# Gate products, single-token expert lists and input squares moved between stages and engines of a hybrid decoder block

## Chip, cores and metric

One core of one Trainium2 chip runs the whole block. The metric is device microseconds from start to end; lower is better. The time before is 1631.74 us, the median of 3 runs (1631.34 to 1634.24).

## What is computed

One layer for 256 tokens of width 2048, all in float32 at the interface:

```python
xn = rms_norm(x)
q, k, v, z, xbc, dt = split(xn @ w_in)
attn = rms_norm(stick_breaking_attention(rms_norm(q), rms_norm(k), v))
y = group_rms_norm(ssd_scan(silu(conv(xbc)), dt, ...) * silu(z))
h = x + concat(attn, y) @ w_out
hn = rms_norm(h)
q = (hn @ w_query).reshape(t, 8, 2, 128)
top_s, top_i = top_k(q . sub_keys, 16)          # per head and half
gate, expert = softmax(top16(top_s0 + top_s1)), key pair of 16384
out = h + sum_e gate_e * gelu(hn . expert_down[e]) * expert_up[e]
```

The last line is what the change touches most: each of the 256 tokens picks 16 of 16384 experts for each of 8 heads, and every expert has one row of 2048 numbers in `expert_down` and one in `expert_up`.

## The kernel before

Nothing is gathered per token. After the query the kernel sorts the used experts into **lists** of 128 experts each; one indirect DMA (L1355) brings a list's 128 rows of 2048 numbers, 1.05 MB, into SBUF. There are kinds of lists by how many tokens use an expert. A list of many-token experts is multiplied against tokens on TensorE (PE) after its rows have been transposed there. An expert that one token alone uses needs just one dot product; 30 lists hold such experts, and they are called **D lists** here.

The program is one long list `items`. `stream` walks over it: for each item it first issues the front part of the items a few places ahead (loads, transposes), then the item's matmuls, then a tick that advances every background generator in `bg` by one step and counts down the callbacks in `due`. The order of each engine's instructions follows from this walk and from the tile scheduler, which may still move them. The stages are:

1. Input projections: x arrives in 8 loads, ACT (L343) and VectorE (DVE, L344) split it with its gain into a rounded part and a rest, ACT and DVE (L222, L227) do the same with weights, and PE multiplies (L312, L313, L318). The mean square of x comes from four `Square`s of a quarter each (L2034, L2036), three sums (L2039) and a matmul. `squares` does two squares and two sums on GpSimd (POOL), two squares on ACT and one sum on DVE. Of the constant tables, two are loaded by POOL's own DMA queue (L422 and L428, together 0.66 MB).
2. Attention and scan, output projection, query, top-16 selection, listing.
3. **C units**, 20 lists of 4 items each, PE only on long matmuls (L1540 to L1542). Beside them runs `gates`: it turns the chosen experts and weights into a dense table of gates, 4 tokens at a time: one-hot tiles on DVE and POOL (L1246 to L1249), a product on PE (L1256), a copy on ACT (L1259), and at each half eight stores to a DRAM table `g_dram` (L1264). `GR` is how many such groups start per item. The expert rows go into a ring of five slots.
4. **T units**, 22 of them (numbered from 0 here), each a pair of lists in 8 items: transposes (L1465), ACT and DVE splits (L1442, L1443), matmuls (L1482 to L1484). Beside them run three things. `turn_hn` transposes the normalised hidden state (64 transposes, L1641) from unit `HU`; `form` fetches a list's gates from `g_dram` (L1420) and multiplies them in, from unit `GU`; and from unit `DU` on, `DN` D lists are zipped into T units. For a D list, `d_prep` fetches the gates, `find` (L1563 to L1565, 5 items later) finds on DVE which token each expert belongs to, `turn_` makes a one-hot matrix of it, 8 matmuls (L1609) pick the right token's hidden state for each row, and 4 DVE operations (L1615) form the dot products with the gathered rows.
5. The **D/up stage** (1182 to 1340 us): four more ring slots open (`begin`), and the D lists that are left are mixed with the first 29 lists of `expert_up` rows, whose halves ACT and DVE split (L1828, L1829) and PE multiplies into the output (L1895).
6. The late up lists, the same without D lists, to the end.

Row gathers, gate fetches and POOL's other work share POOL's one instruction stream. A row gather waits for a ring slot, and everything behind it on POOL waits with it. The gathers come in the order of the list `gathers`: the pair of a T unit, then a D list's rows, then the next pair. The few lines that set the order:

```python
HU, GU, DU, DN = 5, 9, 11, 11       # T unit of turn_hn, of form, first unit with a D list; D lists in T units
        n = i - DU
        if 0 <= n < DN:
            u = [x for p in zip(u[:4], dus[n]) for x in p] + u[4:]
    for n in range(DLOOK):
        after(1 + 3 * n, lambda n=n: d_prep(n))
```

Of the kernel before, what the change touches and what calls it, by code (L numbers as in the profile page):

```python
# [13 lines left out]
AF = mybir.ActivationFunctionType  # L14
OP = mybir.AluOpType
# [54 lines left out]
BASE = [sum(CAPS[:k]) for k in range(LC + 1)]  # L70
# [20 lines left out]
YR = 2  # L91
YC = 2
YT = 2
GR = 0.8
KP = 0
GW = 3
GLAG = 1
# [1 line left out]
OLAG = 7  # L99
TF = 10  # L100
XZ = 16
HU = 5
GU = 9
DU = 11
DN = 11
NPG = 4
YF = 3
HNP = 16
# [35 lines left out]
def tile_block(ctx: ExitStack, tc: tile.TileContext, xT, w_f, w_v, w_dt, w_o, w_q, sk, dnt, down, up,  # L144
               cols, hcols, cst, sel, sel2_, out):
    nc = tc.nc
# [63 lines left out]
    bg = []  # L210
# [46 lines left out]
    def after(n, fn):  # L257
        due.append([n, fn])
# [981 lines left out]
    def gates():  # L1240
# [32 lines left out]
        while t0 < T or q:  # L1273
            if gens.get("put"):
                gens["put"].pop(0)()
                yield from rest(GW if t0 < T else GX)
                continue
            credit += GR
            while q and (len(q) > GLAG or t0 == T):
# [39 lines left out]
    ts_ = plain[:TF] + buffered + plain[TF:]  # L1319
# [19 lines left out]
    gathers = []  # L1339
# [209 lines left out]
    d_list = sorted(d_of, key=d_of.get)  # L1549
# [157 lines left out]
    t_mark = len(items)  # L1707
    u_mark = []
    dus = [unit_d(k, r) for _, k, r in ds_]
    for i, (_, k, r) in enumerate(ts_):  # L1710
        u_mark.append(len(items))
        u = unit_t(k, r)
        n = i - DU
        if 0 <= n < DN:
            u = [x for p in zip(u[:4], dus[n]) for x in p] + u[4:]
        items.extend(u)
        if 0 <= n - 1 < DN:
            gathers.append(("down", d_list[n - 1]))
        gathers += [("down", BASE[k] + r + x) for x in range(2)]
    if len(ts_) - DU <= DN:  # L1720
        gathers.append(("down", d_list[len(ts_) - DU - 1]))
    d_mark = len(items)


# [281 lines left out]
    sqw = [slot(1, 1024 * q, 1024) for q in range(4)]  # L2006
# [23 lines left out]
    def squares():  # L2030
        for q in range(4):
            xq = xt_t[:, 1024 * q:1024 * (q + 1)]
            if q < 2:
                nc.gpsimd.tensor_tensor(sqw[q], xq, xq, op=OP.mult)  # L2034
            else:
                nc.scalar.activation(sqw[q], xq, AF.Square)  # L2036
                yield
            if q:
                (nc.gpsimd if q < 3 else nc.vector).tensor_tensor(sqw[0], sqw[0], sqw[q], op=OP.add)  # L2039

    sq_ = squares()
    next(sq_)
    bg.append(sq_)
    for k, n in enumerate(CL):
        after(n, lambda k=k: load_consts(k))
    stream(items, wo_mark)
# [14 lines left out]
    bg.append(gens["hnt"])  # L2061
    stream(items, u_mark[GU])
    while gens["hnt"] in bg:
# [2 lines left out]
    gens["form"] = form()  # L2066
    bg.append(gens["form"])
    for n in range(DLOOK):
        after(1 + 3 * n, lambda n=n: d_prep(n))
    stream(items, d_mark, d_mark)  # L2070
    pgs.extend(pg_all[NPG:])
    begin()
# [90 lines left out]
```

## Time and profile before

| | |
|---|---|
| median of 3 runs | 1631.74 us |
| profiled execution, its time | 1630.61 us |
| its span in the profile | 1628.7 us |
| TensorE busy | 1580.7 us, 97% |
| VectorE busy | 1156.0 us, 71% |
| ScalarE busy | 779.5 us, 48% |
| GpSimd busy | 531.1 us, 33% |
| mean granted clock | 0.997 |
| moved by DMA | 366.70 MB, mean 225 GB/s |

The profiled execution is the one from which all durations come. Its time is 1.9 us longer than the span that the profile covers, and 1.1 us below the median of the runs. An engine's share is an average over stages with different limits, so the views by stage and the waits say more than the table.

### The profile page before, as it was taken

What the parts mean: (1) busy time and instruction counts of PE and PEld (TensorE: products, weight loads), DVE (VectorE), ACT (ScalarE), POOL (GpSimd) and SP (SyncE); (2) the same over time, 40 slices, a digit from 0 to 9 for tenths busy, and PEclk for the clock granted to TensorE, in tenths of its full rate; (3) what the DMA queues carried; (4) which work ended last, traced back from release to release, by engine and by line L of the source; (5) the groups of instructions that cost most, each with busy time, mean ns of one, the idle gap of its engine ahead of it and who ended that gap; (6) DMA issues with size and microseconds to landing.
All of it is one profiled execution on the core that took longest, in us unless ns stands there. A gap on an engine that the chain in (4) does not pass through costs nothing. (4 is left out here: it accounts for less than half of the span.)

```text
span 1628.7 us, 27340 instructions
## 1 busy us (share of the span) xinstructions
PE 1580.7 (97%) x10330; PEld 1402.2 (86%) x10331; DVE 1156.0 (71%) x2556; ACT 779.5 (48%) x1375; POOL 531.1 (33%) x499
## 2 busy tenths in 40 slices
PE   6999999999999999999999999999998999999997
PEld 6999978999888888889999999999975468887776
DVE  7776665864487988736645774677797457888896
ACT  6554457754111200415545566655552036667664
POOL 3001100211000000034423431455576555786851
PEclk9999999999999999999999999999999999999999
DMA  6654544667745534253294269678799998898893
GB/s 207 188 163 151 156 155 141 183 201 225 244 143 149 164 90 119 66 198 120 96 292 171 79 229 340 227 288 307 284 398 413 356 383 332 322 347 304 327 334 115
DMA packets 108808, 366.70 MB, mean 225 GB/s; under 512 B 12704, under 2 KB 48800, under 8 KB 82304
## 3 DMA queue, kind: packets, MB, share of 16 engines
q0 software_dynamic: 35504, 229.43, 37.7%
q1 hardware_dynamic: 70304, 134.23, 27.0%
q8 instruction: 83, 1.36, 0.3%
q10 hardware_dynamic: 2864, 1.24, 0.3%
q14 instruction: 53, 0.43, 0.1%
HBM read 337.24 MB, written 27.92 MB: 224 GB/s over the span
## 5 line engine op out<-in xcount | busy, mean ns | idle before, releaser
L1895 PE MATMUL out<-hi_up,p 128*128 128x512 f32 x716 | 194.0, 392 | 0.7 <-DVE p L1797 0.6
L1355 POOL DMA_INDIRECT raws<-in_down,idx x71 | 72.3, 1018 | 303.8 <-DVE colt L1196 161.9
L1895 PEld LDWEIGHTS out<-hi_up,p 128*128 128x128 f32 x716 | 133.8, 188 | 30.7 <-ACT hi_up L1828 1.5
L253 PE MATMUL dn<-xt_t,raw_dn 128*128 128x256 f32 x640 | 158.3, 383 | 0.1
L1443 DVE TENSOR_TENSOR t<-tp,t 128x512 fp32r<-128x512 f32 x176 | 120.0, 688 | 48.3 <-ACT t L1442 47.6
L1420 POOL DMA_INDIRECT raw_small<-g_dram,idx x111 | 123.5, 1113 | 43.5 <-issue 28.7
L1442 ACT ACTIVATE t<-tp 128x512 fp32r<-128x512 f32 x176 | 103.8, 602 | 59.7 <-PE tp L1465 57.0
L253 PEld LDWEIGHTS dn<-xt_t,raw_dn 128*128 128x128 f32 x640 | 115.2, 193 | 11.7 <-issue 0.5
L253 PE MATMUL pq<-hg,raw_pq 128*128 128x256 f32 x512 | 112.9, 379 | 0.0
L253 PEld LDWEIGHTS pq<-hg,raw_pq 128*128 128x128 f32 x512 | 96.3, 190 | 12.5
L1259 ACT ACTIVATE big<-g 128x128 f32<-128x128 f32 x256 | 70.8, 438 | 75.8 <-PE g L1256 75.8
L1248 POOL TENSOR_TENSOR B<-B,gi 128x512 bf16<-128x512 bf16 x64 | 69.7, 1091 | 91.1 <-DVE B L1246 89.9
L1465 PE MATMUL tp<-ident,raws 128*128 128x128 f32 x544 | 95.5, 273 | 2.2 <-DVE t L1443 2.2
L1540 PE MATMUL zc<-hnl,c 128*128 128x256 f32 x320 | 95.9, 300 | 0.0
L1828 ACT ACTIVATE hi_up<-raws 128x1024 fp32r<-128x1024 f32 x74 | 77.1, 1056 | 32.7 <-PE out L1895 29.3
L1542 PE MATMUL zc<-hnl,c 128*128 128x256 f32 x320 | 89.1, 278 | 0.0
L1541 PE MATMUL zc<-hnl,c 128*128 128x256 f32 x320 | 89.0, 278 | 0.0
L1828 ACT ACTIVATE hi_up<-rows_hn 128x1024 fp32r<-128x1024 f32 x68 | 71.1, 1059 | 34.7 <-PE out L1895 29.4
L1443 DVE TENSOR_TENSOR c<-tc,c 128x512 fp32r<-128x512 f32 x80 | 55.2, 691 | 43.3 <-ACT c L1442 43.3
L1249 DVE TENSOR_TENSOR A<-O,gi 128x1024 f16<-128x1024 bf16 x64 | 47.4, 741 | 52.0 <-PE g L1256 51.8
L1829 DVE TENSOR_TENSOR lo_up<-rows_hn,hi_up 128x1024 fp32r<-128x1024 f32 x58 | 71.2, 1234 | 13.3 <-ACT hi_up L1828 10.5
L1355 POOL DMA_INDIRECT rows_hn<-in_up,idx x48 | 63.0, 1312 | 46.7 <-DVE lo_up L1829 12.9
(540 smaller groups left out, 4628.4 us busy)
## 6 DMA issues: line engine op xcount, KB each, us to landing
raw_dn<-in_dnt SPq DMA_DIRECT2D x40, 512.0 KB, 3.9
raw_kq<-in_w_f SPq DMA_DIRECT2D x32, 512.0 KB, 3.8
raw_wo<-in_w_o SPq DMA_DIRECT2D x32, 512.0 KB, 4.5
raw_pq<-in_w_q SPq DMA_DIRECT2D x32, 512.0 KB, 3.8
g_dram<-big SPq DMA_DIRECT2D x16, 1024.0 KB, 14.7
raw_xb<-in_w_f SPq DMA_DIRECT2D x22, 512.0 KB, 4.4
raw_v<-in_w_v SPq DMA_DIRECT2D x16, 512.0 KB, 3.6
raw_z<-in_w_f SPq DMA_DIRECT2D x16, 512.0 KB, 3.8
```

What stands on the lines that cost most here:

```text
L253: nc.tensor.matmul(acc, raw[:, j * P:(j + 1) * P], mv[:, k * 8 + j, :], start=(k + j == 0), stop=(k * 8 + j == ND - 1))
L1355: g = nc.gpsimd.indirect_dma_start(out=where[what, j], out_offset=None, in_=down_rows if what == "down" else up_rows, in_offset=bass.Indir ...
L1420: nc.gpsimd.indirect_dma_start(out=dst, out_offset=None, in_=g_half if w == P else g_dram, in_offset=bass.IndirectOffsetOnAxis(ap=idx[:, 1 ...
L1442: a = nc.scalar.activation(hi, tp, AF.Copy).ins
L1443: d = nc.vector.tensor_tensor(lo, tp, hi.bitcast(F32), op=OP.subtract).ins
L1465: nc.tensor.transpose(tp[:, (2 * dd + i) * P:(2 * dd + i + 1) * P], row("down", j + i)[:, d * P:(d + 1) * P], ident)
L1540: nc.tensor.matmul(z, wh, ah[:, d, :], start=(d == 0), stop=False)
L1541: nc.tensor.matmul(z, wh, al[:, d, :], start=False, stop=False)
L1542: nc.tensor.matmul(z, wl, ah[:, d, :], start=False, stop=(d == ND - 1))
L1828: marks["act"] = nc.scalar.activation(hi, raw, AF.Copy).ins
L1829: marks["dve"] = nc.vector.tensor_tensor(lo, raw, hi.bitcast(F32), op=OP.subtract).ins
L1895: nc.tensor.matmul(oa[tt][2 * hf + c], w[:, k * P:(k + 1) * P], mv[:, c * 512:(c + 1) * 512], start=(i == starts[f, tt, hf] and mv is hi a ...
```

## The change

`GR` goes from 0.8 to 1.0, `HU` from 5 to 3, `GU` from 9 to 5, `DU` from 11 to 7 and `DN` from 11 to 19. A T unit may now take two D lists, the second zipped into its items 4 to 7. Unit `i` gets two while the D lists left outnumber the units left: by that rule units 7, 8, 9 and 10 get two each and units 11 to 21 one each, 8 + 11 = 19. So 11 D lists are left for the D/up stage, where there were 19. The first four gate fetches of D lists are 6 items apart, where they were 3. All four squares move to ACT and all three sums to DVE, and they run as a background generator.

```diff
-GR = 0.8
+GR = 1.0
...
-HU = 5
-GU = 9
-DU = 11
-DN = 11
+HU = 3
+GU = 5
+DU = 7
+DN = 19
...
+    left = list(range(DN))
     for i, (_, k, r) in enumerate(ts_):
         u_mark.append(len(items))
         u = unit_t(k, r)
-        n = i - DU
-        if 0 <= n < DN:
-            u = [x for p in zip(u[:4], dus[n]) for x in p] + u[4:]
+        gathers += [("down", BASE[k] + r + x) for x in range(2)]
+        more = 2 if len(left) > len(ts_) - i else 1
+        for x in range(more if i >= DU else 0):
+            n = left.pop(0)
+            gathers.append(("down", d_list[n]))
+            u[8 * x:8 * x + 4] = [v for p in zip(u[8 * x:8 * x + 4], dus[n]) for v in p]
         items.extend(u)
-        if 0 <= n - 1 < DN:
-            gathers.append(("down", d_list[n - 1]))
-        gathers += [("down", BASE[k] + r + x) for x in range(2)]
-    if len(ts_) - DU <= DN:
-        gathers.append(("down", d_list[len(ts_) - DU - 1]))
...
     def squares():
         for q in range(4):
             xq = xt_t[:, 1024 * q:1024 * (q + 1)]
-            if q < 2:
-                nc.gpsimd.tensor_tensor(sqw[q], xq, xq, op=OP.mult)
-            else:
-                nc.scalar.activation(sqw[q], xq, AF.Square)
+            nc.scalar.activation(sqw[q], xq, AF.Square)
+            if q:
+                nc.vector.tensor_tensor(sqw[0], sqw[0], sqw[q], op=OP.add)
+            if q > 1:
                 yield
-            if q:
-                (nc.gpsimd if q < 3 else nc.vector).tensor_tensor(sqw[0], sqw[0], sqw[q], op=OP.add)
-
-    sq_ = squares()
-    next(sq_)
-    bg.append(sq_)
+
+    bg.append(squares())
...
     for n in range(DLOOK):
-        after(1 + 3 * n, lambda n=n: d_prep(n))
+        after(1 + 6 * n, lambda n=n: d_prep(n))
```

Three places show how the built program moves. POOL's first instructions before (`odd` and `sel` are constant tables, `big` the squares, `xp` an edge of the convolution):

```order
L436 IOTA odd 128x512
L2034 TENSOR_TENSOR big_70<-xt_t 128x1024 x2
L438 CAST iota<-odd 128x512
L2039 TENSOR_TENSOR big_70<-big_70 128x1024
L456 MEMSET xp_283 128x3
L422 DMA odd<-in_sel 96x2048
L2039 TENSOR_TENSOR big_70<-big_70 128x1024
L423 MEMSET odd 128x256
L456 MEMSET xp_328 128x3
L428 DMA odd<-in_sel_ 128x1024
```

And with the change:

```order
L436 IOTA odd 128x512
L456 MEMSET xp_283 128x3
L422 DMA odd<-in_sel 96x2048
L438 CAST iota<-odd 128x512
L423 MEMSET odd 128x256
L456 MEMSET xp_328 128x3
L428 DMA odd<-in_sel_ 128x1024
```

The four arithmetic operations are gone, and the two table loads have nothing but short fills and a cast ahead of them.

ACT in the same stretch, before (`hi_first` and `hi_xb` are the rounded weights of the first items) and then with the change:

```order
L222 ACTIVATE hi_first_111<-raw_first_91 128x1024
L343 ACTIVATE xhl<-xt_t,colt 128x256 x8
L2036 ACTIVATE big_70<-xt_t 128x1024
L222 ACTIVATE hi_first_131<-raw_first_92 128x1024
L343 ACTIVATE xhl<-xt_t,colt 128x256 x4
L222 ACTIVATE hi_xb_0_149<-raw_xb_0_147 128x1024
L2036 ACTIVATE big_70<-xt_t 128x1024
```

```order
L222 ACTIVATE hi_first_111<-raw_first_91 128x1024
L343 ACTIVATE xhl<-xt_t,colt 128x256 x8
L222 ACTIVATE hi_first_131<-raw_first_92 128x1024
L343 ACTIVATE xhl<-xt_t,colt 128x256 x4
L222 ACTIVATE hi_xb_0_145<-raw_xb_0_143 128x1024
L2032 ACTIVATE big_70<-xt_t 128x1024 x3
L222 ACTIVATE hi_xb_1_183<-raw_xb_1_181 128x1024
```

The square that stood ahead of the second `hi_first` is now behind the first `hi_xb`, with two others.

DVE in the T units, before in the first unit with a D list (unit 11, `t60` is its split tile; `raws` is a ring slot, `xt0` and `xt1` the picked hidden states):

```order
L1615 SCALAR_TENSOR_TENSOR raws_6921,dsc_11256<-raws_6921,xt0_11482 128x512
L1565 SCALAR_TENSOR_TENSOR raw_small0_10659,dsc_11256<-raw_small0_10659,iota_76 128x128
L1443 TENSOR_TENSOR t60_1_11500<-tp60_1_11495,t60_1_11500 128x512
L1615 SCALAR_TENSOR_TENSOR raws_6921,dsc_11256<-raws_6921,xt1_11483 128x512
L1615 SCALAR_TENSOR_TENSOR raws_6921,dsc_11256<-raws_6921,xt0_11482 128x512
L1443 TENSOR_TENSOR t60_2_11527<-tp60_2_11522,t60_2_11527 128x512
L1673 TENSOR_TENSOR xa2_7256<-xa2_7256,raw_small0_10659 128x128
L1443 TENSOR_TENSOR t60_3_11552<-tp60_3_11547,t60_3_11552 128x512
L1615 SCALAR_TENSOR_TENSOR raws_6921,dsc_11256<-raws_6921,xt1_11483 128x512
L1443 TENSOR_TENSOR t60_4_11570<-tp60_4_11565,t60_4_11570 128x512
```

With the change, in unit 8, the second of the units with two D lists (`xa2` is the fifth ring slot):

```order
L1443 TENSOR_TENSOR t69_2_11203<-tp69_2_11198,t69_2_11203 128x512
L1615 SCALAR_TENSOR_TENSOR raws_6921,dsc_10775<-raws_6921,xt1_10988 128x512
L1615 SCALAR_TENSOR_TENSOR raws_6921,dsc_10775<-raws_6921,xt0_10987 128x512
L1443 TENSOR_TENSOR t69_3_11225<-tp69_3_11220,t69_3_11225 128x512
L1615 SCALAR_TENSOR_TENSOR raws_6921,dsc_10775<-raws_6921,xt1_10988 128x512
L1673 TENSOR_TENSOR raw_zr_7209<-raw_zr_7209,raw_small0_10418 128x128
L1615 SCALAR_TENSOR_TENSOR xa2_7303,dsc_10775<-xa2_7303,xt0_10987 128x512
L1443 TENSOR_TENSOR t69_4_11245<-tp69_4_11240,t69_4_11245 128x512
L1615 SCALAR_TENSOR_TENSOR xa2_7303,dsc_10775<-xa2_7303,xt1_10988 128x512
L1443 TENSOR_TENSOR t69_5_11265<-tp69_5_11260,t69_5_11265 128x512
L1615 SCALAR_TENSOR_TENSOR xa2_7303,dsc_10775<-xa2_7303,xt0_10987 128x512
```

Four operations of one D list are followed at once by those of a second one, among the same eight splits of the unit.

## Rows read from the trace of the kernel before

**Rows 1.** The page, part 1: busy us, share of the span, instructions.
```profile
PE 1580.7 (97%) x10330; PEld 1402.2 (86%) x10331; DVE 1156.0 (71%) x2556; ACT 779.5 (48%) x1375; POOL 531.1 (33%) x499
```

**Rows 2.** Windows by stage: stretch, length, busy us by engine, PEclk, DMA share, GB/s.
```profile
680.00:960.00 280.00, 280.00 (x2252) 270.47 (x2250) 172.25 (x339) 135.39 (x390) 101.35 (x93) 1.00 0.46 157
1040.00:1180.00 140.00, 134.56 (x1072) 128.53 (x1072) 103.53 (x271) 78.32 (x155) 73.66 (x78) 1.00 0.78 284
1180.00:1240.00 60.00, 52.72 (x224) 38.95 (x223) 57.73 (x143) 28.11 (x48) 43.53 (x38) 1.00 1.00 403
1240.00:1340.00 100.00, 95.33 (x294) 54.59 (x295) 54.51 (x167) 17.63 (x32) 54.48 (x55) 0.98 0.97 378
```

**Rows 3.** Timeline of DVE, 0 to 32 us: start, length, operation, idle before.
```profile
5.06 3.31 DVE L344 SCALAR_TENSOR_TENSOR xhl<-xt_t,colt,xhl 128x256 fp32r<-128x256 f32 x4 [4.18 <-ACT xhl L343]
9.43 10.07 DVE L344 SCALAR_TENSOR_TENSOR xhl<-xt_t,colt,xhl 128x256 fp32r<-128x256 f32 x8
20.56 1.66 DVE L344 SCALAR_TENSOR_TENSOR xhl<-xt_t,colt,xhl 128x256 fp32r<-128x256 f32 x4
```

**Rows 4.** Timeline of POOL, 0 to 32 us.
```profile
5.13 2.17 POOL L2034 TENSOR_TENSOR big<-xt_t 128x1024 f32<-128x1024 f32 x1 [3.31 <-DMA xt_t<-in_xT]
14.49 0.74 POOL L422 DMA_DIRECT2D odd<-in_sel  x1
17.83 0.59 POOL L428 DMA_DIRECT2D odd<-in_sel_  x1
```

**Rows 5.** Timeline of PE, 0 to 32 us.
```profile
8.29 0.58 PE L312 MATMUL xb<-xhl,hi_first 128*128 128x256 f32 x1 [8.29 <-ACT hi_first L222]
17.97 0.58 PE L313 MATMUL xb<-xhl,hi_first 128*128 128x256 f32 x1 [2.33 <-DVE xhl L344]
24.08 0.28 PE L312 MATMUL xb<-xhl,hi_xb 128*128 128x256 f32 x1
```

**Rows 6.** Windows of 2 us in the start; columns as in rows 2.
```profile
10.00:12.00 2.00, 0.98 (x5) 0.69 (x4) 2.00 (x2) 2.00 (x5) 2.00 (x3) 1.00 1.06 413
14.00:16.00 2.00, 0.80 (x2) 0.50 (x2) 2.00 (x2) 2.00 (x5) 1.98 (x4) 1.00 0.12 31
```

**Rows 7.** DMA view, 0 to 30 us: POOL's queue; packets, MB, engines' share.
```profile
q0 software_dynamic: 256, 0.66, 13.1%
```

**Rows 8.** Tile view of big, 940 to 1035 us: starts, landing.
```profile
L1264 SPq DMA_DIRECT2D g_dram<-big x8: 360/6000/9754, 960.5 to 995.7; - x8
DMA to landing us min/median/max: 5.2/15.7/21.6
```

**Rows 9.** Timeline of POOL, 955 to 1120 us.
```profile
973.29 0.94 POOL L1355 DMA_INDIRECT raws<-in_down,idx  x1 [7.14 <-PE tp L1465]
982.66 0.94 POOL L1355 DMA_INDIRECT raws<-in_down,idx  x1 [7.18 <-PE tp L1465]
1029.59 0.95 POOL L1420 DMA_INDIRECT raw_small<-g_dram,idx  x1 [0.30 <-issue]
1081.89 0.94 POOL L1355 DMA_INDIRECT raws<-in_down,idx  x1 [2.52 <-DVE raws L1615]
1093.30 0.94 POOL L1355 DMA_INDIRECT raws<-in_down,idx  x1 [2.83 <-DVE raws L1615]
```

**Rows 10.** Timeline of PE, 1203 to 1205 us.
```profile
1203.66 0.63 PE L1609 MATMUL xe<-hnt,ot 128*128 128x512 f32 x2
1204.13 0.62 PE L1895 MATMUL out<-lo_up,p 128*128 128x512 f32 x2
```

**Rows 11.** Lines by form, DVE, 1060 to 1180 us: busy, mean, idle before.
```profile
L1615 DVE SCALAR_TENSOR_TENSOR raws<-raws,xt 128x512 f32<-128x512 f32 x40 | 27.3, 685 | 19.5 <-PE xt L1609 11.7 <-DMA raws<-in_down,idx 5.3 <-PE tp L1465 2.5
```

**Rows 12.** DMA view, 1050 to 1180 us: issues, median us to landing.
```profile
raws<-in_down,idx POOLq DMA_INDIRECT x25, 6.5
```

**Rows 13.** Waits of DVE, 1050 to 1182 us: total us, times, longest.
```profile
DVE raws L1615 <- DMA raws<-in_down,idx: 5.3, 5, 1.9
```

**Rows 14.** DMA view, 1180 to 1240 us: POOL's queue.
```profile
q0 software_dynamic: 3587, 24.15, 99.4%
```

## Prediction

> **What bounds the kernel now.** I read the page first, then the windows by stage, then the timelines and waits of the stages that the change touches. TensorE (PE) is busy 97% of the span [rows 1], so work that is only moved from one PE-bound stage to another gains nothing; a gain must come from places where PE stands idle. The windows [rows 2] show where that is. In the C units PE is busy 280.0 of 280 us. In the T units it is 134.6 of 140. In the D/up stage it is 52.7 of 60 and then 95.3 of 100: 12.0 us idle, the largest hole after the start. In the first 60 us of that stage VectorE (DVE) is busy 57.7 of 60 us and the DMA engines are full (share 1.00, 403 GB/s), nearly all of it POOL's gather queue [rows 14]; in the next 100 us DVE falls to 55% and DMA stays at 0.97. So the stage is bound by DVE and DMA together at first, by DMA and PE later.
>
> The other hole is the start. DVE does four splits of x in 1.66 us when it is alone, but took 3.31 us for the first four and 10.07 us for the next eight [rows 3], which alone would take some 3.3: 1.65 + 6.75 = 8.4 us lost. All of it falls in the time from 5.13 to 17.8 us, in which POOL does its two squares and two sums [rows 4]. PE starts at 8.29, waits for those splits, the last time for 2.33 us up to 17.97, and reaches the next item at 24.08 [rows 5].
>
> **Squares on ACT.** POOL's four operations go, and with them DVE's loss. Without it DVE would end the eight splits at 9.43 + 3.3 = 12.7, the second weight split (1.2 us) at 13.9 and the last four at 15.6, where they end at 20.56 + 1.66 = 22.2 now: 6.6 us earlier. PE is behind DVE by 1.9 us at the end (24.08 against 22.2), so 6.6 us is the most that the start can give. ACT's four squares stand behind the first `hi_xb` and delay only weights of later items, for which PE comes at 24 us today; the three DVE sums (1.2 us each) lie behind all splits of x. I cost both at nothing; the cover is PE's own 5 us or so per item, and if it failed, one 1.0 us square would show.
>
> What can take the gain back: the two table loads on POOL's queue stood behind POOL's arithmetic and were issued at 14.49 and 17.83 [rows 4], when DMA was nearly idle (share 0.12 from 14 to 16 us) [rows 6]. Now nothing holds them back, and they go out at 1 to 3 us, among x's loads and the first weights, where DMA is full (1.06) [rows 6]. They cost 13.1% of 30 us = 3.9 us of all 16 engines [rows 7]. If all of that falls ahead of the last x and weight, the gain is 6.6 - 3.9 = 2.7; if half, 4.6. I take **-3.5** between the two, with ends 0 and -6.6.
>
> A rule speaks against this part of the change: the Trainium skill, "DMA: Bandwidth & Descriptors", section "Queues, rings and completion order", says that a DMA engine goes round-robin between the queues that have work, packet by packet. By it the tables get their turns from the start, however many loads of x are queued, and the gain is the 2.7; no row here shows two queues full at once in the start.
>
> **Gates faster, forming earlier.** `GR` packs the same one-hots into fewer items. Its cover is PE, busy for all of the C units, where DVE has 172 and ACT 135 of 280 us [rows 2]; a quarter more per item keeps DVE under 78%. Cost 0. The gates end 16 items earlier (64 groups of 4 tokens, 64/0.8 = 80 items against 64), which is at least 16 x 1.2 us = 19 us with T items (9.4 us a unit, 8 items). The eight stores were issued up to 995.7 and took 15.7 us to land in the median [rows 8], to 1011.4, so to 992 now. Forming begins 4 T units earlier, so its first gate fetch comes at 1029.6 - 4 x 9.4 = 992 instead of 1029.6 [rows 9]. That is close: the first fetch waits on POOL for the stores, and the row gathers queued behind it wait too. The margin before was 18 us. I take **+1**, ends 0 and +3. Transposing the hidden state two units earlier moves the same 64 transposes between full PE stretches: 0.
>
> **D lists in T units.** A pure T unit takes 982.66 - 973.29 = 9.4 us, one with a D list 1093.30 - 1081.89 = 11.4 [rows 9]. That is PE's price of a D list: two of its matmuls take 0.47 us [rows 10], eight 1.9, and the one-hot's transposition 0.1, in all 2.0 us. Eight lists move, so 16 us of PE work enter the T units and 16 leave the D/up stage: 0 in sum, and the table is made from what goes beyond it.
>
> In the four double units PE needs 9.4 + 2 x 2.0 = 13.4 us. DVE has 103.5 of 140 us today [rows 2], 8.6 us in a unit; a D list adds four operations of 0.685 [rows 11] and its `find`, some 3.5 us: 12.1, or 90% of 13.4. So DVE fits, but with little room for waiting. And it will wait. Five ring slots hold a unit's pair, its two D lists and one row of the next pair. The next unit's other row takes the slot of the first D list, which comes free in good time; but its first D list gets the slot of a T row, which is released at the unit's last transposes, about 4 us before DVE wants the rows (three items), while a gather lands in 6.5 us [rows 12]. Already with one D list DVE waits for such rows, 5 times, up to 1.9 us [rows 13]. So 2.5 us of wait on DVE against 1.3 us of room, and the T splits behind it on DVE are what PE needs next. I take +1.5 a unit, **+6**; ends 0 (PE's queue covers it, as mostly today) and +3.5 a unit, +14.
>
> **The D/up stage.** Eight of 19 D lists leave it: 16 us of PE, 28 us of DVE, 8 x 1.05 = 8.4 MB. If DMA sets the time, the stage ends 8.4 MB / 403 GB/s = 20.8 us earlier, 4.8 beyond PE's 16. If all of PE's idle time goes, 12.0 beyond. In the first stretch, if four of the eight leave it, DVE needs 57.7 - 14 = 44 us and DMA (24.2 - 4.2 MB)/403 GB/s = 50 us, so DMA is the nearer limit; but the gathers that were crowded in there now have the T units, where the share is 0.78. I take **-8**; ends -4.8 and -12. The late up lists keep their work: 0.
>
> **Sum.** -3.5 + 1 + 6 - 8 = -4.5 against the profiled execution's 1630.6: 1626.1. The median of the runs is 1.1 above that execution, so the forecast is **1627.0**.
>
> **Rivals.**
> - *Slower: the double units starve.* If the row of the D list is late by most of its landing time and PE has no transposed tile in store because the splits stand behind the waiting operation on DVE, a unit loses 6.5 - 2 = 4.5 us: +18, and with the other terms (-10.5) +7.5, some 1639. It decides from (10.5 + 3.3)/4 = 3.5 us a double unit on. For it: the waits that are there with one D list [rows 13] and DVE at 90%. Against it: these cost PE 5.4 us in 140 in all [rows 2]. Chance 0.19.
> - *No change: both gains are given back.* The tables take the whole start gain, and the D/up stage stays bound by DMA: 0 + 1 + 6 - 4.8 = +2.2, 1632 to 1634. For it: full DMA in both places [rows 2, 6]. Chance 0.27. The skill's rule on the queues belongs here: by it the start gives 2.7, and the sum is -0.5, 1631.2.
> - *Larger gain.* The tables fit between the loads and the double units cost nothing: -6.6 + 1 + 0 - 10 = -15.6, 1616. Chance 0.10.
> - That the change does not do what it says: the second list is in the first four units from 7 on, not the last four, but the sum above is made for that order. No chance of its own.
>
> **Chances and range.** The forecast's own case has 0.44. A measurement of this kernel can tell about 0.2%, 3.3 us, from no change. Faster by more than that: 0.44 + 0.10 = 0.54; within it 0.27; slower 0.19. The sum of the low ends is -18.6 and of the high ends +12.2 (1613 and 1644); the range 1616 to 1638 leaves a tenth at either side.
>
> **What would show it.** Start: POOL's table loads before 4 us, DVE's eight splits of x in 3.3 us, PE's next item at 20 to 21.4 us rather than 24.08 (17.5 if the tables don't matter, 24 if they take all). T units: gathers of D rows 13.4 to 17 us apart per double unit, DVE's wait for rows at L1615 above 5.3 us. D/up stage: 24 us shorter, DVE no longer full, DMA near 400 GB/s. First gate fetch near 992 with a wait for the stores under 3 us. The forecast is wrong if the double units take over 16.9 us, if the first item is not earlier, or if the stage after the T units gives less than 20 us.

## The result and the profile after

The changed kernel takes **1617.8 us** (median of four runs), the kernel before 1631.9 us beside it: a ratio of 0.9907 [0.9888, 0.9927], so 0.9% faster. Three of them took 1616.1 to 1618.4 us; the fourth, a slow one of 7753.1 us that nothing here explains, is left out of the ratio. The profiled execution took 1618.38 us. The experiments behind it ran on four chips, and on three of them the kernel before took 1646 to 1652 us; which chip the first runs had is not on record. So every run is given as a ratio to the kernel before on its own chip, and times are compared only within one chip.

The page of the changed kernel, part 1, answers to [rows 1]:

```profile
PE 1578.9 (98%) x10330; PEld 1403.3 (87%) x10331; DVE 1155.1 (71%) x2558; ACT 781.3 (48%) x1377; POOL 510.9 (32%) x495
```

The work is the same to 2 us on every engine but POOL, which gave up its four operations of squares. The time came out of PE's idle stretches. The windows by stage (columns as in [rows 2]) show where:

```profile
680.00:960.00 280.00, 280.00 (x2256) 270.78 (x2255) 174.45 (x334) 137.23 (x396) 101.56 (x93) 1.00 0.52 171
...
1040.00:1180.00 140.00, 136.94 (x1058) 128.45 (x1059) 110.30 (x299) 77.33 (x156) 76.75 (x81) 1.00 0.83 308
1180.00:1240.00 60.00, 57.37 (x295) 45.63 (x293) 53.00 (x114) 33.94 (x55) 39.04 (x35) 1.00 0.92 363
1240.00:1340.00 100.00, 95.36 (x315) 57.19 (x314) 50.25 (x129) 22.79 (x33) 53.11 (x51) 0.98 0.99 392
```

The C units are as full as before. From 1180 to 1240 us PE is busy 57.37 of 60 us, where it had 52.72; but 16 us of that stretch are T units now, since these end at 1195.9 us and not at 1180.6. Of the D/up stage alone, the first 60 us were (1181 to 1241 us before, 1196 to 1256 now)

```profile
1181.00:1241.00 60.00, 52.05 (x217) 38.09 (x215) 57.51 (x149) 28.43 (x48) 43.56 (x37) 1.00 1.00 403
```
```profile
1196.00:1256.00 60.00, 55.26 (x224) 40.60 (x223) 53.98 (x118) 31.43 (x49) 39.28 (x34) 0.97 0.98 396
```

so DVE is no longer full, and DMA still is, nearly. The stretch from 1040 to 1180 us, which now holds the last 25 of the 60 us of units with two D lists (1005 to 1065 us) and ten units with one, is fuller as well (136.94 against 134.56).

**The start.** DVE's splits of x, from its timeline (start, length, operation, idle before):

```profile
11.16 0.89 DVE L344 SCALAR_TENSOR_TENSOR xhl<-xt_t,colt,xhl 128x256 fp32r<-128x256 f32 x2 [0.53 <-ACT xhl L343]
12.59 2.48 DVE L344 SCALAR_TENSOR_TENSOR xhl<-xt_t,colt,xhl 128x256 fp32r<-128x256 f32 x6 [0.55 <-ACT xhl L343]
...
16.91 1.66 DVE L344 SCALAR_TENSOR_TENSOR xhl<-xt_t,colt,xhl 128x256 fp32r<-128x256 f32 x4
```

Eight splits take 0.89 + 2.48 = 3.37 us, where they took 10.07 [rows 3]. POOL's timeline has the two table loads at once:

```profile
1.81 0.71 POOL L422 DMA_DIRECT2D odd<-in_sel  x1
...
3.35 0.59 POOL L428 DMA_DIRECT2D odd<-in_sel_  x1
```

And PE starts later, but reaches the next item earlier (19.75 us, 24.08 before [rows 5]):

```profile
9.43 0.58 PE L312 MATMUL xb<-xhl,hi_first 128*128 128x256 f32 x1 [9.43 <-ACT hi_first L222]
...
19.75 0.28 PE L312 MATMUL xb<-xhl,hi_xb 128*128 128x256 f32 x1
```

**The gates and the first fetch.** The tile view of `big` (the stores to `g_dram`), and POOL's timeline around the first gate fetch:

```profile
L1264 SPq DMA_DIRECT2D g_dram<-big x8: 359/3596/9645, 932.9 to 970.6; - x8
...
DMA to landing us min/median/max: 5.2/17.8/28.2
```
```profile
985.22 0.94 POOL L1355 DMA_INDIRECT raws<-in_down,idx  x1 [0.30 <-DMA g_dram<-big]
986.51 0.95 POOL L1420 DMA_INDIRECT raw_small<-g_dram,idx  x1 [0.34 <-issue]
```

The stores went out 25 us earlier than in [rows 8], and the first fetch at 986.5 us (1029.6 before, [rows 9]) lost next to nothing to them: the gather just ahead of it waited 0.30 us for the stores.

**Stage by stage.** PE's own order gives a ledger: the end of the T units is its last matmul of L1482 to L1484; the D/up stage lasts from there until the first output matmul (L1894, before the change L1895) of the 30th list of up rows, the late lists from there to the last output matmul. In microseconds of the two profiled executions:

| step | before | after | difference |
|---|---|---|---|
| PE reaches the second item | 24.08 | 19.75 | -4.3 |
| PE ends the output projection (last L318) | 407.94 | 403.94 | -4.0 |
| end of the T units | 1180.6 | 1195.9 | +15.3 |
| length of the D/up stage | 163.9 | 139.4 | -24.5 |
| length of the late lists | 275.7 | 272.6 | -3.1 |

The third line holds 16 us of D lists that left the D/up stage (eight by 2.0, the difference between units of 11.4 and 9.4 us), and -4.0 from the start, so the T units and what lies ahead of them stalled 15.3 + 4.0 - 16 = 3.3 us more than before. In the same way -24.5 is -16 of moved work and -8.5 of stalls. (By windows over the D/up stage, 1181 to 1344 and 1196 to 1335 us, PE's busy time fell by 18.1 us and its idle time from 12.0 to 6.1, so some 2 us of the 8.5 are busy time.) The sum is -4.0 + 3.3 - 8.5 - 3.1 = -12.3, against 1630.61 - 1618.38 = 12.2 measured.

The length of a T unit (from its first L1465 on PE to the next unit's) will be needed throughout. Units 7 to 10 are those with two D lists after the change; before, units from 11 on have one.

| kernel | chip: before takes | unit 5 | 6 | 7 | 8 | 9 | 10 | 11 | 12 | 13 |
|---|---|---|---|---|---|---|---|---|---|---|
| before | 1632 | 11.6 | 12.8 | 10.7 | 9.4 | 9.4 | 9.5 | 14.4 | 12.5 | 11.4 |
| changed | 1632 | 10.7 | 9.5 | 15.6 | 13.8 | 15.1 | 15.2 | 13.0 | 11.8 | 11.4 |
| changed, again | 1652 | 15.0 | 10.6 | 17.0 | 19.7 | 16.8 | 22.3 | 19.2 | 16.2 | 16.9 |
| one list a unit | 1652 | 15.0 | 10.7 | 14.0 | 12.1 | 12.5 | 12.3 | 12.7 | 12.5 | 12.4 |

The last two rows are two of the experiments below, on one chip.

### The profile page after: what moved, and what is told of

The parts are those of the page before. It is cut to its first block, busy times and chain, and to the rows that moved or that the text cites. A ratio compares the mean times of both kernels' runs of the same rounds, so it can differ in the third digit from the quotient of the medians.

```text
span 1616.5 us, 27319 instructions
## 1 busy us (share of the span) xinstructions
PE 1578.9 (98%) x10330; PEld 1403.3 (87%) x10331; DVE 1155.1 (71%) x2558; ACT 781.3 (48%) x1377; POOL 510.9 (32%) x495
## 4 chain that ended last, share of the span: by engine, by line
PE 89%; DVE 5%; DMA 3%; issue 1%; ACT 1%; POOL 0%; SPq 0%; DVEq 0%; ACTq 0%; POOLq 0%
PE out L1894 21%; PE pq L253 7%; PE dn L253 7%; PE tp L1465 4%; PE g L1256 4%; PE v L735 3%; PE zc L1540 2%; PE zc L1541 2%; PE zc L1542 2%; PE z L1483 2%; PE tc L1523 2%; PE z L1484 2%; PE z L1482 2%; PE kq L312 2%; PE wo L318 2%; PE cnt L1057 2%
## 5 line engine op out<-in xcount | busy, mean ns | idle before, releaser
L1894 PE MATMUL out<-hi_up,p 128*128 128x512 f32 x716 | 193.2, 392 | 2.2 <-ACT hi_up L1827 2.2
L1894 PEld LDWEIGHTS out<-hi_up,p 128*128 128x128 f32 x716 | 134.0, 189 | 31.9 <-ACT hi_up L1827 3.9
L1443 DVE TENSOR_TENSOR t<-tp,t 128x512 fp32r<-128x512 f32 x176 | 119.7, 688 | 58.3 <-ACT t L1442 57.7
L1420 POOL DMA_INDIRECT raw_small<-g_dram,idx x111 | 119.8, 1080 | 42.5 <-issue 26.6
L253 PEld LDWEIGHTS dn<-xt_t,raw_dn 128*128 128x128 f32 x640 | 115.1, 193 | 11.6 <-issue 0.5
L253 PEld LDWEIGHTS pq<-hg,raw_pq 128*128 128x128 f32 x512 | 96.3, 190 | 12.5
L1465 PE MATMUL tp<-ident,raws 128*128 128x128 f32 x624 | 100.4, 273 | 1.3 <-DMA raws<-in_down,idx 1.0
L1443 DVE TENSOR_TENSOR c<-tc,c 128x512 fp32r<-128x512 f32 x80 | 55.1, 690 | 39.5 <-ACT c L1442 39.1
L1894 PE MATMUL out<-lo_up,p 128*128 128x512 f32 x254 | 76.9, 395 | 1.8 <-DVE lo_up L1828 1.8
L1355 POOL DMA_INDIRECT raws<-in_up,idx x49 | 60.8, 1241 | 53.7 <-DVE lo_up L1828 17.2
```

What stands on the lines that cost most here:

```text
L253: nc.tensor.matmul(acc, raw[:, j * P:(j + 1) * P], mv[:, k * 8 + j, :], start=(k + j == 0), stop=(k * 8 + j == ND - 1))
L1355: g = nc.gpsimd.indirect_dma_start(out=where[what, j], out_offset=None, in_=down_rows if what == "down" else up_rows, in_offset=bass.Indir ...
L1420: nc.gpsimd.indirect_dma_start(out=dst, out_offset=None, in_=g_half if w == P else g_dram, in_offset=bass.IndirectOffsetOnAxis(ap=idx[:, 1 ...
L1443: d = nc.vector.tensor_tensor(lo, tp, hi.bitcast(F32), op=OP.subtract).ins
L1465: nc.tensor.transpose(tp[:, (2 * dd + i) * P:(2 * dd + i + 1) * P], row("down", j + i)[:, d * P:(d + 1) * P], ident)
L1894: nc.tensor.matmul(oa[tt][2 * hf + c], w[:, k * P:(k + 1) * P], mv[:, c * 512:(c + 1) * 512], start=(i == starts[f, tt, hf] and mv is hi a ...
```

## The experiments

Theory: a gain from the start and a larger one from the D/up stage, of which the units with two D lists give a part back. Rival: these units cost as much as the stage after them gives.

### The squares alone

The kernel before, with this part of the change alone:

```diff
-            if q < 2:
-                nc.gpsimd.tensor_tensor(sqw[q], xq, xq, op=OP.mult)
...
+            nc.scalar.activation(sqw[q], xq, AF.Square)
+            if q:
+                nc.vector.tensor_tensor(sqw[0], sqw[0], sqw[q], op=OP.add)
```

> The kernel before with only the squares moved to ACT and their sums to DVE. My theory: the start is worth what the changed kernel shows there, first new item at 19.75 instead of 24.08 us, and that 4.0 us carries to the end because every later stage is PE-bound: 1627.5 to 1628.5 against 1631.8, with the T units, the D/up stage (161 us) and the late lists (278 us) as before. Rival: the start only shifts the waits of later stages and under 1 us is left at the end (1631).

1639.6 us against 1647.1: 0.9958 [0.9935, 0.9981]. The output projection ended at 403.3 us, and D/up stage (166.1) and late lists (275.9) are those of the kernel before within 2.2 us. The start's gain is real and stays to the end. The 7.5 us are more than the 4.0 that were expected, but the interval, 3.1 to 10.7 us, holds both.

### The lists and gates without the squares

The changed kernel, with the squares of the kernel before:

```diff
-            nc.scalar.activation(sqw[q], xq, AF.Square)
...
+            if q < 2:
+                nc.gpsimd.tensor_tensor(sqw[q], xq, xq, op=OP.mult)
```

> The changed kernel with the squares as before, two on POOL. My theory: the parts add, so 8 to 10 us faster than before, 1622 to 1624, with the first new item back at 24.1 us, the double T units at about 15 us, the D/up stage at 137 us and the late lists at 275. Rival: squares and lists are not independent (the lists' gain hangs on the earlier start through the gates); then over 1627.

1660.3 us on the same chip: 1.0082 [1.0056, 1.0107], slower than before, where 8 to 10 us faster was expected. With POOL's squares back, eight splits of x on DVE take 8.43 us again:

```profile
11.70 8.43 DVE L344 SCALAR_TENSOR_TENSOR xhl<-xt_t,colt,xhl 128x256 fp32r<-128x256 f32 x8
```

The four double units took 16.9, 17.8, 16.7 and 22.6 us here, 74.0 in all, where the changed kernel had 59.7 in the first runs. That is the rival's case, on another chip.

### The tables held back

The changed kernel, with one line ahead of the first table load and its like ahead of the second, so that POOL waits for the last load of x:

```diff
+            nc.gpsimd.tensor_copy(selt[0:1, 0:1], xt[0:1, ND - 1, 0:1])
```

> The changed kernel with the two table loads made to wait, on POOL, for the last load of x (a copy of one number of it into each table's first place, which the load then overwrites). My theory: in the changed kernel the tables' 0.66 MB go out at 1.8 and 3.4 us among x's loads and make the first weights and x late (PE starts at 9.43 instead of 8.29 us); held back they cost nothing, PE starts at 8.2 to 8.4 us and reaches the next item at 17.5 to 18.3 us instead of 19.75: 1.5 to 2.2 us faster than the changed kernel, some 1615.5. Rival: the loads of x and of the first weights are slow by themselves, and the next item stays at 19.5 to 20.

1651.9 us: 1.0025 [1.0003, 1.0046]. POOL now issues the loads behind the last x:

```profile
14.11 0.71 POOL L423 DMA_DIRECT2D odd<-in_sel  x1
14.81 0.61 POOL L430 DMA_DIRECT2D odd<-in_sel_  x1
```

and PE begins the stage behind the output projection at 400.87 us, in the next run on the same chip, with the tables early, at 403.20:

```profile
400.87 0.59 PE L253 MATMUL pq<-hg,raw_pq 128*128 128x256 f32 x2
```
```profile
403.20 0.38 PE L253 MATMUL pq<-hg,raw_pq 128*128 128x256 f32 x1
```

So by this pair the tables at the head of the queue cost 2.3 us. At the second item it is 2.7 us: PE reaches it at 16.54 us here and at 19.20 in the next run, where the loads of x land 8.3 us after their issue in the median, 5.6 here. Still, this kernel is a little slower than the one before: the double units took 16.8, 17.6, 16.7 and 22.1 us again.

### One D list a unit

The changed kernel with 15 D lists in units 7 to 21, none double:

```diff
-DN = 19
+DN = 15
```

> The changed kernel with 15 D lists in the T units, one each in units 7 to 21, no double units, 15 in the D/up stage. My theory: a double unit takes 15 us where 13.4 would do, some 6 us over four units; four lists fewer leave the D/up stage, which at 8.6 us of relief for eight is 4.3 us. So single units are 1 to 3 us faster than the changed kernel or equal, 1615 to 1618. Rival: the double units' loss is the first units' start-up and not the doubling, it stays; then 3 to 5 us slower than the changed kernel, 1621 to 1623.

1632.6 us: 0.9914 [0.9892, 0.9936], so 19 us faster than the run with the tables held back and 28 faster than the one without the squares, all on one chip. The expectation was 1 to 3 us or nothing. Units with one D list took 11.9 to 13.9 us.

### The changed kernel again, on another chip

The kernel itself, without an edit.

> The changed kernel once more, as the yardstick beside the next three and beside the kernel before. In the last four runs the kernel before took 1647 us instead of 1632, and engines of all kinds showed short idle times in the T units that end at nothing the profile shows (issue); double units took 17 to 22 us there instead of 15. Theory 1: what the change gives depends on those stalls, so where the kernel before takes 1632 this one gives 1616 to 1618, and where it takes 1647 this one is at 1645 to 1655, no gain. Theory 2: the double units' 17 to 22 us came from the edits of those runs alone; then 14 us faster than the kernel before in both cases.

1664.6 us against 1651.9: **1.0055 [1.0031, 1.0079], slower**. The windows (columns as in [rows 2]):

```profile
1040.00:1180.00 140.00, 119.82 (x804) 108.24 (x804) 88.16 (x239) 60.57 (x126) 60.39 (x63) 0.90 0.63 231
1180.00:1240.00 60.00, 55.95 (x429) 51.43 (x428) 41.74 (x112) 25.67 (x54) 30.30 (x33) 1.00 0.75 281
```

PE is busy 119.8 of 140 us, and the granted clock is at 0.90: part of the stretch ran at 1.2 GHz, which follows on PE's idle pieces. On the mean DVE (88 of 140) and DMA (0.63) are no bound either. Everybody waits for somebody. Two of POOL's waits between 1040 and 1180 us (total, times, longest):

```profile
POOL xa L1355 <- DVE xa L1615: 31.2, 6, 8.2
POOL raw_small L1420 <- DVE zc L1680: 11.5, 1, 11.5
```

A D list's row gather waits for DVE to be done with the slot, and a gate fetch (L1420) for a gate buffer. POOL's timeline at the start of unit 10:

```profile
1062.29 0.96 POOL L1420 DMA_INDIRECT raw_small<-g_dram,idx  x1 [5.74 <-DVE xa L1673]
1063.55 0.96 POOL L1355 DMA_INDIRECT raws<-in_down,idx  x1 [0.31 <-issue]
...
1066.08 0.95 POOL L1355 DMA_INDIRECT raws<-in_down,idx  x1 [0.30 <-issue]
1067.34 0.95 POOL L1355 DMA_INDIRECT raws<-in_down,idx  x1 [0.30 <-issue]
```

and PE's, at the same place:

```profile
1068.37 0.27 PE L1465 MATMUL tp<-ident,xa 128*128 128x128 f32 x1
1074.88 0.69 PE L1498 MATMUL z<-ident,zt 128*128 128x128 f32 x2 [6.24 <-issue]
1075.36 0.42 PE L1465 MATMUL tp<-ident,raws 128*128 128x128 f32 x1
```

The fetch stood 5.74 us, row gathers went out behind it, and PE stood 6.2 us until about the time at which they were in; the transposes (L1465) behind that wait take 0.42 us, at the lower clock, where they took 0.27. The next gate fetch stood longer still:

```profile
1084.81 0.95 POOL L1420 DMA_INDIRECT raw_small<-g_dram,idx  x1 [11.46 <-DVE zc L1680]
```

Windows of 4 us show what the mean of 0.63 hides:

```profile
1070.00:1074.00 4.00, 0.00 (x0) 0.00 (x0) 0.00 (x0) 0.00 (x0) 2.73 (x3) 0.85 0.99 383
...
1078.00:1082.00 4.00, 4.00 (x29) 3.87 (x28) 3.46 (x10) 1.89 (x5) 0.00 (x0) 0.80 0.02 4
1082.00:1086.00 4.00, 4.00 (x31) 3.64 (x29) 3.74 (x10) 1.24 (x3) 0.95 (x1) 1.00 0.00 0
...
1090.00:1094.00 4.00, 0.83 (x5) 0.37 (x3) 0.21 (x3) 0.10 (x1) 3.08 (x4) 0.91 0.92 311
```

While POOL stands, DMA runs empty (0.02, 0.00); then the gathers behind the fetch come in one burst, DMA is full (0.99, 0.92), and PE, DVE and ACT stand, wholly or nearly, until rows are in. PE's wait itself has no releaser in the trace ("issue"), so this is a reading, not a proof.

### One D list a unit, on the same chip

The edit of e4_single.

> 15 D lists, one each in units 7 to 21, beside the changed kernel this time. Theory 1: single units leave room for late rows, so this kernel keeps its gain (14 to 15 us faster than the kernel before) whatever the stalls; against the changed kernel it is within 2 us where the kernel before takes 1632, and 10 us or more faster where it takes 1647. Theory 2: within 2 us of the changed kernel in both cases.

1636.5 us: 0.9897 [0.9865, 0.9929], 28 us faster than the changed kernel beside it. So it is the double units that lose on this chip. The windows:

```profile
1040.00:1180.00 140.00, 134.00 (x1010) 123.29 (x1009) 100.10 (x256) 72.77 (x150) 68.22 (x72) 0.99 0.76 276
1180.00:1240.00 60.00, 55.68 (x320) 46.39 (x319) 49.94 (x120) 30.53 (x56) 36.84 (x34) 1.00 0.85 326
```

PE is back at 134.0 of 140 us, at a clock of 0.99.

### Gates and squares, D lists as before

The changed kernel with the D lists where the kernel before has them:

```diff
-DU = 7
-DN = 19
+DU = 11
+DN = 11
```

> The changed kernel with the D lists where they were, 11 in units 11 to 21 and 19 in the D/up stage; gates, forming and squares as changed. If the late lists' 3 us came from forming that is done sooner (fewer gate fetches left for the late stage), they show here (275 instead of 278 us), and the first units with a D list lose their 14.4 and 12.5 us (11.4 each): 4 + 3 + 3 = 10 us faster than before with the D/up stage at its old 161 us. Rival: the 3 us came from the shorter D/up stage; then only the start's 4 us and about 2 us in the T units, 6 us faster.

1643.4 us: 0.9945 [0.9928, 0.9962]. The D/up stage took 165.9 us and the late lists 275.2, as before the change. So the faster gates and the earlier forming give nothing to those stages; what they gained needs the D lists moved. The 0.55% can't be told from what the squares give alone (0.9958 [0.9935, 0.9981]).

### The double units last

```diff
-        more = 2 if len(left) > len(ts_) - i else 1
+        more = 2 if i >= len(ts_) - (DN - (len(ts_) - DU)) else 1
```

This gives units 18 to 21 two lists instead of 7 to 10.

> The changed kernel with the double units last, units 18 to 21, and one list each in units 7 to 17. Theory: the double units' price is the slot of the next unit's first D list, released by the T pair; it is the same at the end, 15 us a unit, and forming runs less beside them, so 0 to 3 us faster than the changed kernel. Rival: at the end the gathers of the D/up stage are already asked for, the ring of five is shared with them, and the last units become slower: 2 to 5 us slower than the changed kernel.

1655.2 us: 1.0000 [0.9972, 1.0028], 9.5 us less than the changed kernel beside it (1.0055 [1.0031, 1.0079]), where 3 at most were expected, but no gain over the kernel before. Units 18 to 20 took 16.0, 15.5 and 18.8 us. Its window from 1180 to 1240 us:

```profile
1180.00:1240.00 60.00, 39.28 (x214) 32.00 (x214) 31.60 (x97) 16.14 (x37) 29.90 (x31) 0.81 0.74 277
```

The stretches at half clock in it (0.81 over 60 us) begin at 1207 us, behind these three units, and lengthen the D/up stage, 155.6 us here against 137.8 in the changed kernel beside it. Doubles at the end cost less than doubles at the start, but they are not the remedy: they starve as well, right before the D/up stage.

### One D list a unit, tables held back

The edits of e4_single and e3_tables_late together.

> Single units (15 D lists, units 7 to 21) and the table loads held until the last of x has landed. Theory: the two act at different places and add: single units 14 to 15 us faster than the kernel before, the late tables another 2.3 us at the start (output projection's end at 400.9 instead of 403.2 us, as between the two runs with late and early tables on one chip): 1.0 to 1.1% faster than before, the fastest kernel so far. Rival: the 2.3 us are lost again in the T units, whose rows set their pace; then no faster than single units alone (0.86 to 1.03%).

1630.8 us against 1646.3 on a third such chip: 0.9895 [0.9871, 0.9919]. The output projection ended at 401.8 us. The interval overlaps that of e4_single, so the 2.3 us of the tables can't be told from nothing in the whole time.

### D lists packed into two items

```diff
-            u[8 * x:8 * x + 4] = [v for p in zip(u[8 * x:8 * x + 4], dus[n]) for v in p]
+            a_, d_ = u[8 * x:8 * x + 2], dus[n]
+            u[8 * x:8 * x + 2] = [a_[0], d_[0], d_[1], a_[1], d_[2], d_[3]]
```

Here with one list a unit. By the code this leaves a wait out: the walk issues matmuls three items ahead, and now the third and fourth piece of a list write the two PSUM banks before DVE's operations on the first two are issued, so these use another piece's hidden state. The number of operations is the same.

> Single units with each D list's four pieces zipped into two items of its T unit, not four. Theory: a unit with one D list turns in a loop, row gather (6.0 us from its issue to the rows), then the four dot-product operations of DVE spread over 5.4 to 5.9 us, whose last one frees the slot for the next gather: 11.4 to 12.2 us, as long as PE's 11.4, so it sets the pace wherever PE is a little late. In two items the four take 3 to 4 us, the loop falls to 9 to 10, and a unit takes PE's 11.4 to 11.5: where it took 12.2, some 10 us faster than single units as they were. Rival: PE waits for the two PSUM banks that the four pieces share, and the units stay at 12 or grow.

1646.1 us: 1.0007 [0.9985, 1.0030], 15 us slower than e7_single_late on the same chip (which also holds the tables back), with units of 11.5 to 16.1 us. PE's waits from 1040 to 1180 us:

```profile
PE z L1498 <- ACT zt L1493: 3.4, 3, 2.2
PE tp L1465 <- DVE t L1443: 3.0, 4, 1.2
PE z L1482 <- ACT t L1442: 3.0, 4, 1.7
```

These are splits of ACT and DVE that PE needs, and three or four L1615 now stand in a row on DVE; that these hold the splits up is a reading. The expectation that earlier release cures the units did not come true, but since PE and DVE do not wait for each other here as they would have to, neither packed run decides between its theory and its rival.

The same packing with two lists a unit (the same part of the dot products is changed):

> The changed kernel, 19 D lists with four double units, with each D list's pieces in two items. Theory: the double units' 17 to 22 us come from rows that are asked for too late, since a slot is freed by the last of four spread pieces; packed, the first list's slot is free two items earlier, and the double units take 14 to 16 us: 8 to 20 us faster than the changed kernel beside the same kernel before, so 0.5 to 1% faster than before. Rival: the next unit's first D list still gets a T row's slot, which packing doesn't free any sooner, and the double units stay at 17 to 22.

1658.2 us: 1.0082 [1.0057, 1.0107], where 0.5 to 1% faster than before was expected; the double units took 14.9 to 20.5 us.

### Eight gate buffers

```diff
-NPG = 4
+NPG = 8
```

> The changed kernel with eight gate buffers from the start instead of four, so that POOL's gate fetches need not wait for DVE to free a buffer and the row gathers queued behind them go out at once. Theory: the gate fetches' waits on POOL (5.5 and 5.7 us, seen at 1043 and 1062 us of the changed kernel's second run) hold back row gathers in the units with two D lists; then these units fall from 17 to 22 us to 14 to 16, and the kernel is 8 to 20 us faster against the kernel before than the changed kernel was: ratio 0.993 to 1.000 in place of 1.0055. Rival: the rows are late for another reason (the slots of the gathers themselves); then the ratio stays at 1.003 to 1.008 with units of 17 to 22 us. On a chip where the kernel before needs 1632 us, as in the first runs, the units would stand at 14 to 15.5 us either way and this run would not tell the two apart.

This one met a chip on which the kernel before takes 1631.2 us: 1614.7 us, 0.9891 [0.9855, 0.9927]. As the expectation said for that case, it does not tell theory and rival apart: the interval overlaps that of the changed kernel, 0.9907 [0.9888, 0.9927]. The windows:

```profile
1040.00:1180.00 140.00, 138.89 (x1085) 131.21 (x1084) 112.89 (x305) 79.56 (x161) 79.61 (x84) 1.00 0.85 314
1180.00:1240.00 60.00, 58.22 (x289) 45.28 (x288) 55.54 (x123) 34.98 (x58) 44.29 (x40) 1.00 1.00 394
```

The direction is as the theory has it: the fetches wait for no buffer any more (in the changed kernel's first profile two of them stood 4.05 and 4.43 us at 1045 and 1061 us), the double units took 15.4, 15.1, 14.2 and 14.1 us and unit 11 11.0, 2.9 less in these five, and PE is busy 138.9 of 140 us. What the buffers do where the kernel before takes 1650 us was not tried.

## Why the prediction was right, and where it was not

The forecast was 1627.0 us (1616 to 1638), faster; the result is 1617.8, near the low end. Direction and mechanism held in these runs, and all but 1.5 us of the 9.2 between them lies in the terms: the sum of the terms came out 7.7 us lower than forecast, and the median lies 0.6 us below its profiled execution where 1.1 above was assumed.

- **Squares, -3.5: measured -4.0.** The ceiling of 6.6 us and the tables' price were the two halves of the term. The price is 2.3 us by e3_tables_late against e4_single, and 2.7 at the second item; that 6.6 - 2.3 = 4.3 is just what the second item gained is partly chance, since with the tables held back the item came at 16.5 and 16.8 us, 7.3 to 7.5 earlier than before and not 6.6. By the rule on round-robin service ("DMA: Bandwidth & Descriptors" in the Trainium skill, "Queues, rings and completion order") all 3.9 us would have fallen into the start, by the prediction's estimate; the runs agree that the tables take turns from the loads of x as soon as they are issued, but not with the full price.
- **DVE beside POOL.** The 8.4 us of lost split time were put down to POOL's arithmetic, and with it gone eight splits take 3.37 us; with it back (e2_lists) they take 8.43. The Trainium skill says of this ("SBUF — State Buffer", "SBUF: two separate sides") that VectorE operations with two inputs from SBUF and GpSimd operations that read SBUF exclude each other at a shared port for a whole instruction; 0.41 us a split alone and 1.26 on average in the eight beside POOL [rows 3] agree.
- **First gate fetch, +1: 0.** It came at 986.5 us, not 992, and the gather ahead of it waited 0.3.
- **Moved D lists, 16 us on either side**: this fits both stages, and it cancels.
- **Double units, +6: +6.1, but from a different neighbourhood.** 15.6 + 13.8 + 15.1 + 15.2 = 59.7 against 4 x 13.4 = 53.6. What the term left out is what the units behind them had lost before: units 11 and 12, then the first with a D list, took 14.4 and 12.5 us and take 13.0 and 11.8 now (11.4 is the plain price). So the stages up to the end of the T units lost only 3.3 us, where +1 and +6 were forecast. The reason given for the term is not borne out, so that its size came out right is luck: DVE's waits at L1615 for rows were to rise above 5.3 us, and the waits of DVE from 1050 to 1182 us now read

```profile
DVE xa L1615 <- PE xt L1609: 5.4, 10, 1.0
DVE xa L1615 <- DMA xa<-in_down,idx: 2.5, 3, 1.4
```

 Rows waited for on DMA make 2.5 us, and over the four double units alone (1005 to 1066 us) there is one such wait:

```profile
DVE raws L1615 <- DMA raws<-in_down,idx: 0.9, 1, 0.9
```
 In the first runs the double units lose PE's time in waits of at most 0.7 us, of several kinds.
- **D/up stage, -8: -8.5.** By number of D lists left in it, and without the packed ones, the stage took 164 to 166 us with 19 (three runs), 150 to 154 with 15 (three runs) and 138 to 145 with 11 (five runs, e6_lastfour at its low clock not counted): about 3 us a list, of which 2.0 are PE's work by the price in the T units and the rest stalls. As forecast, DVE is full no more and DMA is (0.98).
- **Late lists, 0: -3.1.** This is the term that was missing. They took 275.2 to 275.9 us in the three runs with 19 D lists left behind the T units and 272.2 to 273.9 in the others, with 15 or 11. POOL's lines from 1340 to 1600 us show it: the gate fetches, 37 before

```profile
L1420 POOL DMA_INDIRECT raw_small<-g_dram,idx x37 | 50.9, 1377 | 11.1 <-issue 10.8 <-DMA rows_hn<-in_up,idx 0.3
```
 and 26 now:

```profile
L1420 POOL DMA_INDIRECT raw_small<-g_dram,idx x26 | 34.5, 1328 | 7.6 <-issue 7.6
```
 The forecast took the late lists as untouched, but fewer gate fetches leave them POOL and DMA time. That this is the cause is argued, not shown: with the gates early and the D lists in their old place (e5_gates) the late lists, counted from their start, held 29 fetches, where the kernel before has 35 and the changed one 26, and took 275.2 us. PE's waits there end mostly at DVE's splits of the up rows, and they make 3.3 us before and 2.0 now, so less than half of the 3.1.
- **The rivals.** The time lies at the number of "Larger gain" (1616, chance 0.10), but not by its conditions: the tables cost 2.3 us and the double units 6.1. "Double units starve" was given 0.19 and 4.5 us a unit, deciding from 3.5 on. In the first runs it stood at 1.5 a unit. On another chip the same kernel lost (75.8 - 53.6)/4 = 5.5 us a double unit, and 18 us more in the three units behind them, and was slower by 0.55%. So the mechanism was named rightly, and its threshold fits; that the chip would decide was not seen. There the prediction fails by its own sign, double units over 16.9 us (19.0 in the mean), and that the first runs fell where they did is luck. One list a unit is faster than before on all three such chips (0.9914, 0.9897, and 0.9895 with the tables held back).

**What stays open** is why the T units with D lists run longer on those chips, also with the D lists where the kernel before has them (mostly 12.2 us in e1_squares, 11.4 in the first runs). Whether it is the chip or the hour isn't known either: no chip is known to have been met twice. Instruction durations (a split of L1443 687 ns against 685) and the stages ahead of the T units are alike. The first slow unit of the changed kernel is the one in which forming begins (unit 5: 15.0 us against 10.7), but e6_lastfour, on the same chip, has 10.7 there. The traces from there hold no landings of the row gathers, so these can't be compared and the first late event can't be named. That double units turn a small delay into a large one is shown; what delays is not.

## What to carry to other kernels

Work moved out of a stage that is bound by two full resources gains more than its own time there, and the next stage may gain as well. How much it costs where it goes depends on slack: a unit in which DVE is busy for five sixths of the time (50.2 of 60 us from 1005 to 1065 us in the changed kernel), with queues that wait on each other, lost 1.5 us on one chip and 5.5 on another, and a gain that rests on it should be measured on more than one chip. The lighter setting (one list a unit) was 0.9 to 1.0% faster on the three chips where it was tried; where the kernel before takes 1632 us it was not. And a mean over a stage can hide that a resource is empty and full by turns: the DMA share of 0.63 was 0.00 and 0.99 within 16 us.

## What was not expected of the hardware

- The same program differed by 1.3% between sets of runs on different chips, 1631 to 1652 us for the kernel before, with instruction durations alike; and a change's sign can differ with it (0.9907 against 1.0055, intervals apart).
- Where PE starves it loses twice: from 1040 to 1180 us the changed kernel's second run had PE busy 119.8 of 140 us and the granted clock at 0.90. A transpose behind its longest wait took 0.42 us, ahead of it 0.27.
- 0.66 MB of tables, at the head of a start full of loads, cost 2.3 us (by one pair of runs) of the 3.9 that they hold all DMA engines [rows 7].
